# The first five z units, the sums of squares and the norm weights of a hybrid decoder block, arranged anew

## The chip, the core and the metric

The kernel runs on one core of a Trainium2 chip. A core has TensorE (PE, matrix products into PSUM), VectorE (DVE), ScalarE (ACT), GpSimd (POOL) and SyncE (SP, which issues transfers), each with its own queue that it works off in order; they meet at semaphores. Operands lie in SBUF, 128 partitions wide; PSUM has eight banks of 128 x 512 float32. The metric is the time of one execution in microseconds (us); smaller is better.

## The reference

One decoder block on 512 tokens of width 1024, batch 1, depth 1, all float32:

```python
u = rmsnorm(x, norm_mix_g)
proj = u @ w_in     # [q_A k_A v_A z_A a_A b_A | q_B k_B v_B f_B | gate_A gate_B]
# A: causal conv(4) + SiLU on q,k,v; q,k L2-normed; beta = sigmoid(b_A)
#    g = -exp(a_log) * softplus(a_A + dt_bias); gated delta rule in chunks -> o_A
y_A = (rmsnorm(o_A, gdn_norm_g) * silu(z_A)) @ w_proj_gdn
# B: per-head QK RMSNorm, log_f = log_sigmoid(f_B + f_bias),
#    softmax(q k^T / sqrt(d) + c_t - c_s), c = cumsum(log_f), causal -> o_B
y_B = o_B @ w_proj_fox
h = x + (sigmoid(gate_A) * y_A + sigmoid(gate_B) * y_B) @ w_out
out = h + relu(rmsnorm(h, norm_mlp_g) @ w_up)^2 @ w_down
```

The change concerns `u`, the 1024 columns of z_A and the 24 columns of a_A, b_A and f_B ("ab").

## The kernel before, in words

Every float32 product is made of three: a value is split into a high part (rounded to the type that TensorE takes in one pass, a cast on ScalarE) and a low part (what the cast left, a subtraction on VectorE), and high x high, high x low and low x high are added in PSUM. x comes transposed, as eight blocks `xt[k]` of 128 channels x 512 tokens; a "unit" of weights is 128 output columns, 128 x 1024 in SBUF, with its eight contraction steps side by side. `load` (L200) issues a unit's transfer, `prefetch_split` (L243) makes its two parts, `unit` (L260) hands it out and keeps both ahead; raw weights have three buffers, the parts four. Transfers go over SP's queue in the order in which the program reaches them. `dense` (L269) makes 24 products of one unit into one PSUM bank; `mmps` (L92) gives out the three banks of the pool `pmm` in rotation, `atps` (L101) those of the other five.

The mean square of a token is only known when all eight blocks are there. So the first part of the projection is made of x times the norm weights `norm_mix_g`, not of u: the loop at L390 splits each block with the weight as scale (L289, L290), squares it on ScalarE (L395) and adds the squares up on VectorE (L397). L400 to L407 go through the eight blocks once for the ab columns (bank 0) and the first two z units (banks 1 and 2). Then `sumsq` (L348) adds over channels with TensorE ("ss"), `inv_rms` (L354) makes 1/rms: scale and offset on VectorE, a power on GpSimd (L345), and a product that spreads it over the partitions ("rb"), copied to SBUF (L364).

After that `normalise` (L410) multiplies each block by rb on GpSimd (L412), splits the result into `uhi` and `ulo` (again L289 and L290) and stores it; `gates` (L467) makes the decay and beta values out of the ab columns, a long chain of small operations with the products "abt", "cum" and "rowsT". Both are generators that advance one piece at each `tick`. Meanwhile `zgate` (L1072) takes z units 2 to 4, still made of x, multiplies by rb (L1081), applies SiLU and stores. From unit 5 on, u is used: the twelve units of the first four DeltaNet heads (`project`, L593, "w_gdn") follow, then the attention branch, the other heads, the projections and the MLP.

A scheduler of the framework sets the order on each engine from the program's order and its own estimates; where two instructions are marked to keep the program's order, it leaves them so.

Of the kernel before, what the change touches and what calls it, by code (L numbers as in the profile page):

```python
# [30 lines left out]
NZX = 5  # L31
# [12 lines left out]
def hybrid_block(tc, a, out):  # L44
# [81 lines left out]

    def tick():
        for t in list(tasks):
            try:
                next(t)  # L130
            except StopIteration:
                tasks.remove(t)
# [67 lines left out]
    def load(n):  # L200
        nme, i = seq[n]
        if nme in FACTOR:
            w, c, s_ = i
            q, old = FACTOR[nme]
            if old is None:
                if w == "w_st":
                    raw = (swp if nme == "P1" else wraw).tile([P, D], F32, tag="raw", name=nm("sraw"))
                else:
                    raw = fresh[2 if nme == "P2" else s_].tile([P, D], F32, tag="raw", name=nm("draw"))
                nc.sync.dma_start(raw, a[w][c, q, s_])  # L210
# [12 lines left out]
        w = 256 if nme == "w_ab" else D  # L223
        raw = wraw.tile([P, D], F32, tag="raw", name=nm("raw"))
        cuts = [slice(0, 512), slice(512, D)] if 0 < n < 3 else [slice(0, w)]
        for c in cuts:
            nc.sync.dma_start(raw[:, c], a[nme][i][:, c])
        raws[n] = raw, cuts
# [14 lines left out]
    def prefetch_split(n):  # L243
        while len(units) < min(len(seq), n):
            raw, cuts = raws[len(units)]
            hi = whl.tile([P, D], F32R, tag="hi", name=nm("hi"))
            if not units:
                h3 = v3(hi[:, 0:512], KT)
                r3 = v3(raw[:, 0:256], KT)
                act.copy(h3[:, :, 0:32], r3)  # L250
                vec.tensor_tensor(h3[:, :, 32:64], r3, h3[:, :, 0:32].bitcast(F32), op=ALU.subtract)
                units.append((hi, None))
                continue
            lo = whl.tile([P, D], F32R, tag="lo", name=nm("lo"))
            for c in cuts:
                act.copy(hi[:, c], raw[:, c])  # L256
                vec.tensor_tensor(lo[:, c], raw[:, c], hi[:, c].bitcast(F32), op=ALU.subtract)  # L257
            units.append((hi, lo))
# [23 lines left out]
    def split(src, scale=None, dst=None):  # L282

        hi, lo = dst or (page(F32R, "hi")[:, :], page(F32R, "lo")[:, :])
        if scale is None:
            act.copy(hi, src)
            vec.tensor_tensor(lo, src, hi.bitcast(F32), op=ALU.subtract)
        else:
            act.activation(hi, src, AF.Copy, scale=scale)  # L289
            vec.scalar_tensor_tensor(lo, src, scale, hi.bitcast(F32),  # L290
                                     op0=ALU.mult, op1=ALU.subtract)
# [12 lines left out]
    for _ in range(NWARM):  # L304
        mm(pw[:, 0:P], ones, ones, start=True, stop=True)
# [42 lines left out]
    def sumsq(sqs):  # L348
        pss = atps("ss")
        for c in range(NCH):  # L350
            mm(pss[:, c * 64:(c + 1) * 64], sqs[:, cs(c)], ones[:, 0:64], start=True, stop=True)
        return pss

    def inv_rms(pss, rs, rb):  # L354


        for c in range(NCH):
            vec.tensor_scalar(rs[:, c:c + 1], pss[:, c * 64:c * 64 + 1], 1.0 / D, EPS, op0=ALU.mult, op1=ALU.add)
# [3 lines left out]
        for c in range(NCH):  # L362
            mm(prb[:, cs(c)], rs[:, c:c + 1].to_broadcast([P, P]), ident, start=True, stop=True)
# [25 lines left out]
    sqs = page(s="proj")  # L389
    for k in range(KT):  # L390
        xs.append(split(xt[k], mix_g[:, k:k + 1], dst=spots[2 * k:2 * k + 2] if k < 3 else None))
        if k < 2:
            prefetch_split(2 + k)
        sq = page(s="sq") if k else sqs
        act.activation(sq, xt[k], AF.Square)  # L395
        if k:
            vec.tensor_tensor(sqs, sqs, sq, op=ALU.add)  # L397
    first = [unit("w_ab"), unit("w_z"), unit("w_z")]
    fps = [mmps() for _ in first]
    for k in range(KT):  # L400
        w = first[0][0][:, k * 64:(k + 1) * 64]
        mm(fps[0][:64, :], w, xh(k), start=(k == 0), stop=False)
        mm(fps[0][:64, :], w, xl(k), start=False, stop=(k == KT - 1))
        for (hi, lo), o in zip(first[1:], fps[1:]):
            mm(o, hi[:, cs(k)], xh(k), start=(k == 0), stop=False)
            mm(o, hi[:, cs(k)], xl(k), start=False, stop=False)
            mm(o, lo[:, cs(k)], xh(k), start=False, stop=(k == KT - 1))  # L407
    pss = sumsq(sqs)
# [58 lines left out]
    def gates(ps):  # L467
        abT = page(s="abT")
        act.copy(abT[:64, :], ps[:64, :])
# [38 lines left out]
        mm(pc[:, 0:64], upper, gf[:, :, :].rearrange("p a b -> p (a b)"), start=True, stop=True)  # L508
# [558 lines left out]


    gt = start(gates(fps[0]))
    tick()  # L1070
    tick()
    def zgate(h):  # L1072
        if h < 2:
            ps = fps[1 + h]
        elif h < NZX:
            ps = dense("w_z", xh, xl)
        else:
            ps = dense("w_z", uh, ul)
        z = page(s="proj")
        if h < NZX:  # L1080
# [440 lines left out]
```

## Time and profile before

| | us |
|---|---|
| median of 3 runs (lowest to highest) | 979.46 (979.27 to 979.87) |
| the profiled execution | 979.09 |
| its span, first to last instruction | 977.3 |

All rows come from this execution, at a granted TensorE clock of 1.00. In a row of the timeline stand the start, the duration, the engine, the line, the operation with output and input, the shapes, the count, and in brackets the idle time before it and who ended it. "PEld" is TensorE's loading of weights, "SPq" SP's queue. `xs`, `hi` and `lo` hold parts of x or of weights, `ulo` the low part of u, `sq` and the first `proj` squares and their sum.

### The profile page before, as it was taken

Reading aid. Unit: us, or ns where it says so; the run is one execution under the profiler, and the core shown is the slowest. Engines: PE = TensorE matmul, PEld = TensorE weight load, DVE = VectorE, ACT = ScalarE, POOL = GpSimd, SP = SyncE. Lnnn points to the kernel's source line nnn. Section 1 sums busy time; section 2 is a strip of 40 time slices with the busy share of each in tenths; the row PEclk is TensorE's granted clock in tenths of the full one; section 3 lists DMA queues with packets and bytes.
Section 4 is the critical chain, followed back from the end, with each engine's and each line's share of the span. In section 5 each row is a group of like instructions: output and inputs, shape, how many; then the busy total and the mean of one; then the engine's idle time right before and its main releaser. Section 6 shows DMA issues by size and latency. Waiting matters only on the chain.

```text
span 977.3 us, 17204 instructions
## 1 busy us (share of the span) xinstructions
PE 968.0 (99%) x6532; PEld 871.9 (89%) x6532; DVE 709.4 (73%) x1206; ACT 617.8 (63%) x1079; POOL 219.5 (22%) x220
## 2 busy tenths in 40 slices
PE   8999999999999999999999999999999999999998
PEld 6788899998888999999998888889989989988986
DVE  6877777656577799855656534889896697698596
ACT  7778654766764787868567412668755765666761
POOL 1503220202313423521320014412121121121110
PEclk9999999999999999999999999999999999999999
DMA  7646872475675987757888726678698888889883
GB/s 267 210 146 191 236 179 88 130 256 175 156 210 163 194 155 169 174 120 175 252 172 234 258 88 191 113 180 173 184 197 192 194 168 203 184 170 205 187 175 110
DMA packets 97634, 176.50 MB, mean 181 GB/s; under 512 B 8160, under 2 KB 53376, under 8 KB 97552
## 3 DMA queue, kind: packets, MB, share of 16 engines
q1 hardware_dynamic: 83088, 122.92, 40.6%
q0 software_dynamic: 14464, 52.49, 30.8%
q8 instruction: 51, 0.84, 0.4%
q14 instruction: 31, 0.25, 0.1%
HBM read 154.34 MB, written 21.04 MB: 179 GB/s over the span
## 4 chain that ended last, share of the span: by engine, by line
PE 91%; ACT 3%; DVE 2%; issue 2%; DMA 1%; POOL 0%; SPq 0%; ACTq 0%; POOLq 0%; DVEq 0%
PE mlp L1172 36%; PE st L1012 13%; PE mm L279 7%; PE mm L276 7%; PE mm L275 7%; PE fx L965 2%; PE fx L962 2%; PE fx L963 2%; PE fo L945 2%; PE sc L920 2%; PE pT L936 1%; ACT hi L256 1%; PE kq L648 1%; PE kk L640 1%; DMA row<-oad 1%
## 5 line engine op out<-in xcount | busy, mean ns | idle before, releaser
L1403 ACT CAST hi<-draw 128x1024 fp32r<-128x1024 f32 x124 | 130.1, 1050 | 118.4 <-PE mlp L1172 101.5
L1410 DVE TENSOR_TENSOR lo<-draw,hi 128x1024 fp32r<-128x1024 f32 x124 | 151.2, 1221 | 44.9 <-ACT hi L1403 42.1
L256 ACT CAST hi<-raw 128x1024 fp32r<-128x1024 f32 (+1 forms) x62 | 62.7, 1020 | 77.6 <-PE mm L276 48.6
L1172 PE MATMUL mlp<-hi,shi 128*128 128x512 f32 x280 | 109.5, 391 | 0.1
L1172 PE MATMUL mlp<-hi,slo 128*128 128x512 f32 x280 | 109.1, 390 | 0.0
L1172 PE MATMUL mlp<-lo,shi 128*128 128x512 f32 x280 | 109.0, 389 | 0.0
L257 DVE TENSOR_TENSOR lo<-raw,hi 128x1024 fp32r<-128x1024 f32 (+1 forms) x62 | 75.4, 1222 | 28.3 <-ACT hi L256 13.6
L1172 PE MATMUL mlp<-slo,hi 128*128 128x256 f32 x448 | 90.3, 283 | 0.0
L1172 PE MATMUL mlp<-shi,lo 128*128 128x256 f32 x448 | 90.3, 283 | 0.0
L1172 PE MATMUL mlp<-shi,hi 128*128 128x256 f32 x448 | 90.3, 283 | 0.0
L276 PE MATMUL mm<-ulo,hi 128*128 128x512 f32 x216 | 84.9, 394 | 1.2 <-DVE ulo L290 1.2
L275 PE MATMUL mm<-uhi,hi 128*128 128x512 f32 x216 | 85.2, 396 | 0.0
L257 DVE TENSOR_TENSOR lo<-sraw,hi 128x1024 fp32r<-128x1024 f32 x49 | 61.6, 1257 | 23.5 <-ACT hi L256 20.1
L1172 PEld LDWEIGHTS mlp<-shi,hi 128*128 128x128 f32 x448 | 70.6, 192 | 0.9
L256 ACT CAST hi<-sraw 128x1024 fp32r<-128x1024 f32 x49 | 51.3, 1047 | 30.7 <-PE st L1012 14.8
L1172 PEld LDWEIGHTS mlp<-shi,lo 128*128 128x128 f32 x448 | 69.9, 192 | 0.0
L1172 PEld LDWEIGHTS mlp<-slo,hi 128*128 128x128 f32 x448 | 69.8, 192 | 0.0
L1172 PEld LDWEIGHTS mlp<-hi,shi 128*128 128x128 f32 x280 | 52.6, 188 | 11.1 <-issue 0.7
L1172 PEld LDWEIGHTS mlp<-lo,shi 128*128 128x128 f32 x280 | 52.6, 188 | 11.1
L1172 PEld LDWEIGHTS mlp<-hi,slo 128*128 128x128 f32 x280 | 52.6, 188 | 10.3
L600 DVE SCALAR_TENSOR_TENSOR conv<-mm,c_conv,conv 128x511 f32<-128x511 f32 (+2 forms) x72 | 53.5, 744 | 5.6 <-ACT conv L597 4.4
L279 PE MATMUL mm<-uhi,lo 128*128 128x512 f32 x216 | 57.1, 402 | 0.0
(337 smaller groups left out, 2389.7 us busy)
## 6 DMA issues: line engine op xcount, KB each, us to landing
draw<-w_u POOLq DMA_DIRECT2D x32, 512.0 KB, 6.0
draw<-w_d POOLq DMA_DIRECT2D x32, 512.0 KB, 6.0
sraw<-w_st POOLq DMA_DIRECT2D x28, 512.0 KB, 6.0
draw<-w_d SPq DMA_DIRECT2D x26, 512.0 KB, 4.3
raw<-w_gdn SPq DMA_DIRECT2D x24, 512.0 KB, 4.3
draw<-w_u SPq DMA_DIRECT2D x24, 512.0 KB, 4.5
sraw<-w_st SPq DMA_DIRECT2D x21, 512.0 KB, 5.2
hd<-hd SPq DMA_DIRECT2D x34, 256.0 KB, 5.5
```

What stands on the lines that cost most here:

```text
L256: act.copy(hi[:, c], raw[:, c])
L257: vec.tensor_tensor(lo[:, c], raw[:, c], hi[:, c].bitcast(F32), op=ALU.subtract)
L275: mm(o, w, rhi(k), start=(k == 0), stop=False)
L276: mm(o, w, rlo(k), start=False, stop=False)
L279: mm(o, lo[:, k * cols:(k + 1) * cols], rhi(k), start=False, stop=(k == KT - 1))
L600: vec.scalar_tensor_tensor(y[:, s:], ps[:, :T - s], cw[:, i:i + 1], y[:, s:], op0=ALU.mult, op1=ALU.add)
L920: mm(psc[:, :n], qT[:, s], kT[:, :n], start=True, stop=True)
L945: mm(po[:, cs(i)], vt[c], st[i][:, cs(c)], start=(c == 0), stop=(c == i))
L1012: mm(o, u, w, start=first and t == 0 and k == 0 and j == 0 and x is hi, stop=x is lo and k == 3, skip_group_check=True)
L1172: return (lambda *args, **kw: tc.keep_in_program_order(f(*args, **kw))) if self.pinned[0] else f
L1403: pact.copy(hi, raws[m][0])
L1410: pvec.tensor_tensor(lo, raws[m][0], hi[:, :].bitcast(F32), op=ALU.subtract)
```

## The change

- The five z units are made side by side. Their weights come as eight blocks `w_zk[k]` of 128 x 640, one for each contraction step with the five units' columns in it (three units as before come later as whole units). Five banks hold the sums: the three of `pmm` and two others; ab has one more. For each k TensorE makes 15 products for z. Those of ab stand ahead of z for k below 4; the other four pairs, `ss` and `rb` are put between z products at fixed places. All of this, and the products `cum` and `rowsT` of the gates, are marked to keep the program's order.
- Squares: GpSimd makes those of blocks 0 to 2 and adds them up, ScalarE the other five, VectorE adds these and the two sums.
- The gates and `normalise` start inside the z loop (`step`), and all five z evictions (`zgate`, now L1140) come after it.
- The norm weights come as 8 rows of 128 over ScalarE's queue and are transposed by TensorE. Six warming products stand ahead of this and three behind it in the program, in place of ten. Before, they came as columns over GpSimd's queue.
- The low parts of the DeltaNet units 2 to 4 (numbers 11 to 13 in `seq`) are made by GpSimd. The ab weights' cast is VectorE's. Small loads, and those of later weights, stay behind the loads of x. `x_id` and `fqs` are made later in the program, and one operation over four columns takes the place of four in `inv_rms`.

Three places where the order moved; names carry a buffer number.

TensorE around the sums of squares. Before (`mm_273` is ab, `mm_274` and `mm_275` are z 0 and 1, `mm_442` z 2):

```order
L403 MATMUL mm_273<-lo_255,hi_200 64x512
L406 MATMUL mm_274<-lo_255,hi_203 128x512
L407 MATMUL mm_274<-hi_254,lo_204 128x512
L406 MATMUL mm_275<-lo_255,hi_212 128x512
L407 MATMUL mm_275<-hi_254,lo_213 128x512
L351 MATMUL ss_340<-ones,proj_197 128x64 x4
L275 MATMUL mm_442<-xs_195,hi_261 128x512
L276 MATMUL mm_442<-xs_195,hi_261 128x512
```

Now (`ab_262` is ab, `mm_263` to `mm_265` and `fp_266` and `fp_267` are the five z units, here at k = 3):

```order
L377 MATMUL ss_364<-ones,proj_200 128x64 x4
L446 MATMUL mm_265<-hi_228,hi_306 128x512
L447 MATMUL mm_265<-lo_229,hi_306 128x512
L448 MATMUL mm_265<-hi_228,lo_307 128x512
L440 MATMUL ab_262<-hi_233,hi_204 64x512
L441 MATMUL ab_262<-lo_234,hi_204 64x512
L446 MATMUL fp_266<-hi_228,hi_306 128x512
L447 MATMUL fp_266<-lo_229,hi_306 128x512
L448 MATMUL fp_266<-hi_228,lo_307 128x512
L440 MATMUL ab_262<-hi_240,hi_204 64x512
L441 MATMUL ab_262<-lo_241,hi_204 64x512
L388 MATMUL rb_381<-ident,rs 128x128 x4
```

`ss` stood behind all products of eight blocks and now stands inside the fourth; ten products follow before `rb`.

VectorE ahead of the first DeltaNet unit. Before:

```order
L1081 TENSOR_TENSOR proj_373<-mm_274,rb 128x512
L1081 TENSOR_TENSOR proj_402<-mm_275,rb 128x512
L477 TENSOR_TENSOR ab<-abt_377,rs 128x128
L1081 TENSOR_TENSOR proj_493<-mm_442,rb 128x512
L482 TENSOR_TENSOR yy<-ab,c_gdn_dt_bias 128x4x8
L483 TENSOR_TENSOR yy<-ab,c_fox_f_bias 128x4x8
L290 SCALAR_TENSOR_TENSOR ulo_185<-x_120,c_norm_mix_g,uhi_177 128x512
L484 TENSOR_SCALAR yy<-yy 128x4x8
L490 TENSOR_SCALAR beta<-beta 128x32
L487 SCALAR_TENSOR_TENSOR ee<-yy 128x64
```

Now (`lo_508` is the low part of DeltaNet unit 1, `mm_263` the bank of z 0, which is the next one that `mmps` gives to DeltaNet unit 0):

```order
L307 SCALAR_TENSOR_TENSOR ulo_192<-x_127,mix_g,uhi_184 128x512
L272 TENSOR_TENSOR lo_508<-raw_473,hi_507 128x1024
L307 SCALAR_TENSOR_TENSOR ulo_193<-x_128,mix_g,uhi_185 128x512
L307 SCALAR_TENSOR_TENSOR ulo_194<-x_129,mix_g,uhi_186 128x512
L520 TENSOR_TENSOR ab<-abt_484,rs 128x128
L307 SCALAR_TENSOR_TENSOR ulo_195<-x_130,mix_g,uhi_187 128x512
L525 TENSOR_TENSOR yy<-ab,c_gdn_dt_bias 128x4x8
L526 TENSOR_TENSOR yy<-ab,c_fox_f_bias 128x4x8
L533 TENSOR_SCALAR beta<-beta 128x32
L527 TENSOR_SCALAR yy<-yy 128x4x8
L534 RECIPROCAL beta<-beta 128x32
L1140 TENSOR_TENSOR proj_551<-mm_263,rb 128x512
```

The first eviction of a z unit stood ahead of all `ulo`, and now stands behind the last one.

GpSimd, from its constants to the multiplication by rb. Before:

```order
L336 COPY mid<-upper 64x128
L337 TENSOR_SCALAR mid<-upper 64x128
L342 TENSOR_SCALAR fqs<-c_fox_q_norm_g 128x1
L345 TENSOR_TENSOR rs<-rs,expo 128x4
L412 TENSOR_TENSOR x_120<-x_120,rb 128x512
L412 TENSOR_TENSOR x_121<-x_121,rb 128x512
```

Now:

```order
L421 TENSOR_TENSOR proj_201<-x_123 128x512
L421 TENSOR_TENSOR sq_220<-x_124 128x512
L423 TENSOR_TENSOR proj_201<-proj_201,sq_220 128x512
L421 TENSOR_TENSOR sq_225<-x_125 128x512
L423 TENSOR_TENSOR proj_201<-proj_201,sq_225 128x512
L1147 TENSOR_SCALAR fqs<-c_fox_q_norm_g 128x1
L371 TENSOR_TENSOR rs<-rs,expo 128x4
L453 TENSOR_TENSOR x_123<-x_123,rb 128x512
L453 TENSOR_TENSOR x_124<-x_124,rb 128x512
L453 TENSOR_TENSOR x_125<-x_125,rb 128x512
```

Five tensor operations of 128 x 512 have come in ahead of the power; behind the eight multiplications there now also stand three subtractions of 128 x 1024.

The diff, cut to its core:

```diff
-NWARM = 10
+NWARM = 6
 NZ1 = 5
+SQA = 3
+POOL_LO = range(11, 14)
...
-    seq = [("w_ab", 0)] + [("w_z", i) for i in range(NZ1)]
+    seq = [("w_ab", 0)] + [("w_zk", k) for k in range(KT)]
...
             for c in cuts:
-                act.copy(hi[:, c], raw[:, c])
-                vec.tensor_tensor(lo[:, c], raw[:, c], hi[:, c].bitcast(F32), op=ALU.subtract)
+                i = act.copy(hi[:, c], raw[:, c])
+                if len(units) < 3:
+                    pin(i)
+                eng = pool if len(units) in POOL_LO else vec
+                eng.tensor_tensor(lo[:, c], raw[:, c], hi[:, c].bitcast(F32), op=ALU.subtract)
...
+    mix_row = page(s="mixr")[0:KT, 0:P]
+    nc.scalar.dma_start(mix_row, a["norm_mix_g"])
...
+    warm_up(NWARM)
+    pg_ = atps("mixg")
+    nc.tensor.transpose(pg_[:, 0:KT], mix_row, ident[0:KT, 0:KT])
+    mix_g = const([P, KT], "mix_g")
+    act.copy(mix_g, pg_[:, 0:KT])
+    warm_up(3)
...
-    mix_g = small_in("norm_mix_g", [P, KT], nc.gpsimd)
+    AHEAD = {0: 2, 1: 3, 3: 4, 7: 5}
     for k in range(KT):
-        nc.sync.dma_start(xt[k], a["xT"][k])
-        if k < 2:
-            prefetch_raw(2 + k)
-    prefetch_raw(4)
+        last = pin(nc.sync.dma_start(xt[k], a["xT"][k]))
+        if k in AHEAD:
+            prefetch_raw(AHEAD[k])
+    anchor.append(last)
...
+    def square(k):
+        sq = sqp if k == 0 else sqs if k == SQA else page(s="sq")
+        if k >= SQA:
+            pin(act.activation(sq, xt[k], AF.Square))
+        else:
+            pool.tensor_tensor(sq, xt[k], xt[k], op=ALU.mult)
+        if 0 < k < SQA:
+            pool.tensor_tensor(sqp, sqp, sq, op=ALU.add)
+        elif k > SQA:
+            vec.tensor_tensor(sqs, sqs, sq, op=ALU.add)
+        if k == KT - 1:
+            vec.tensor_tensor(sqs, sqs, sqp, op=ALU.add)
...
+    abps = atps("ab")
+    fps = [mmps() if i < NMM else atps("fp") for i in range(NZ1)]
+
+    def ab_products(k):
+        w = w_ab[:, k * 64:(k + 1) * 64]
+        pin(mm(abps[:64, :], w, xh(k), start=(k == 0), stop=False))
+        pin(mm(abps[:64, :], w, xl(k), start=False, stop=(k == KT - 1)))
+
+    def z_products(k):
+        hi, lo = unit("w_zk")
+        for i, o in enumerate(fps):
+            pin(mm(o, hi[:, cs(i)], xh(k), start=(k == 0), stop=False))
+            pin(mm(o, hi[:, cs(i)], xl(k), start=False, stop=False))
+            pin(mm(o, lo[:, cs(i)], xh(k), start=False, stop=(k == KT - 1)))
+            yield
...
-        mm(pc[:, 0:64], upper, gf[:, :, :].rearrange("p a b -> p (a b)"), start=True, stop=True)
+        pin(mm(pc[:, 0:64], upper, gf[:, :, :].rearrange("p a b -> p (a b)"), start=True, stop=True))
...
-    gt = start(gates(fps[0]))
-    tick()
-    tick()
+    for k in range(KT):
+        if k < 4:
+            ab_products(k)
+        for i, _ in enumerate(z_products(k)):
+            u = k * NZ1 + i
+            if u == 16:
+                pss = sumsq(sqs)
+                gt = start(gates())
+                step(gt)
+            if 17 <= u < 21:
+                ab_products(u - 13)
+            if u == 21:
+                act.copy(abT[:64, :], abps[:64, :])
+            if u in (18, 32, 36):
+                step(gt)
+            if u > 18:
+                for t in [t for t in tasks if t is not gt]:
+                    step(t)
...
     def zgate(h):
-        if h < 2:
-            ps = fps[1 + h]
-        elif h < NZX:
-            ps = dense("w_z", xh, xl)
-        else:
-            ps = dense("w_z", uh, ul)
+        ps = fps[h] if h < NZ1 else dense("w_z", uh, ul)
         z = page(s="proj")
-        if h < NZX:
+        if h < NZ1:
             vec.tensor_tensor(z, ps, rb, op=ALU.mult)
             ps = z
         act.activation(z, ps, AF.Silu)
         nc.sync.dma_start(zd[h], z)
-        tick()
+        if h >= NZ1:
+            tick()
```

More of the change, by code (lines that the diff above doesn't have):

```diff
@@ L30 @@
 NMM = 3
-NZX = 5
 DECAY_AT = (9, 1)
@@ L62, in hybrid_block, with behind @@
     pat = psx.enter_context(tc.tile_pool(name="pat", bufs=8 - NMM, space=PSUM))
+    pin = tc.keep_in_program_order
+    anchor = []
+    def behind(d):
+        if anchor:
+            order = mybir.DependencyInfo(mybir.DependencyClass.NoSync, mybir.DependencyReason.DATA)
+            tc.add_manual_dep(d.ins, anchor[0].ins.name, order, reason="behind the first loads")
     n_names = [0]
@@ L125, in hybrid_block, with step @@
     tasks = []
+    def step(t):
+        try:
+            next(t)
+        except StopIteration:
+            tasks.remove(t)
     def tick():
         for t in list(tasks):
[L129 to L132, printed above, removed]
+            step(t)
     def finish(*which):
@@ L303, in hybrid_block, with warm_up, small_in @@
     pw = atps("warm")
-    for _ in range(NWARM):
-        mm(pw[:, 0:P], ones, ones, start=True, stop=True)
-    def small_in(name, shape, eng=None):
+    def warm_up(n):
+        for _ in range(n):
+            mm(pw[:, 0:P], ones, ones, start=True, stop=True)
+    warm_up(NWARM)
[4 more added lines that the diff above has]
+    warm_up(3)
+    def small_in(name, shape):
         t = const(shape, "c_" + name)
-        (eng or nc.sync).dma_start(t, a[name])
+        behind(nc.sync.dma_start(t, a[name]))
         return t
@@ L350, in sumsq @@
         for c in range(NCH):
[L351 removed]
+            pin(mm(pss[:, c * 64:(c + 1) * 64], sqs[:, cs(c)], ones[:, 0:64], start=True, stop=True))
         return pss
     def inv_rms(pss, rs, rb):
[L357 to L358 removed]
+        vec.tensor_scalar(rs, v3(pss[:, 0:NCH * 64], NCH)[:, :, 0], 1.0 / D, EPS, op0=ALU.mult, op1=ALU.add)
         rsq(rs, rs)
@@ L388, in hybrid_block @@
         spots += [t[:, i * T:(i + 1) * T] for i in range(n)]
-    sqs = page(s="proj")
+    sqs, sqp = page(s="proj"), page(s="proj")
+    def square(k):
[10 more added lines that the diff above has]
+            vec.tensor_tensor(sqs, sqs, sqp, op=ALU.add)
     for k in range(KT):
-        xs.append(split(xt[k], mix_g[:, k:k + 1], dst=spots[2 * k:2 * k + 2] if k < 3 else None))
+        xs.append(split(xt[k], mix_g[:, k:k + 1], spots[2 * k:2 * k + 2] if k < 3 else None, None if k else pin))
         if k < 2:
             prefetch_split(2 + k)
[L394 to L408, printed above, removed]
+        square(k)
+    w_ab = unit("w_ab")[0]
+    abps = atps("ab")
[11 more added lines that the diff above has]
+            yield
     def normalise():
@@ L465, in rowc, with gates @@
         return t[:, :].unsqueeze(1).to_broadcast([P, NCH, H])
-    def gates(ps):
-        abT = page(s="abT")
-        act.copy(abT[:64, :], ps[:64, :])
+    X_ID = []
+    abT = page(s="abT")
+    def gates():
         yield from inv_rms(pss, rs, rb)
@@ L539, in gates @@
         yield
+        for _ in range(6):
+            yield
         pt = atps("rowsT")
-        nc.tensor.transpose(pt[:32, 0:P], rows[:, 3, :, :].rearrange("p c h -> p (c h)"), ident)
+        pin(nc.tensor.transpose(pt[:32, 0:P], rows[:, 3, :, :].rearrange("p c h -> p (c h)"), ident))
         rowsF = const([32, P], "rowsF")
```

40 lines of the change are left out of this document (24 added, 16 removed).

## The prediction, made before the changed kernel had run

> **What bounds the kernel now.** First the page's busy times and TensorE's waits (microseconds in total, times, longest).
>
> ```profile
> PE 968.0 (99%) x6532; PEld 871.9 (89%) x6532; DVE 709.4 (73%) x1206; ACT 617.8 (63%) x1079; POOL 219.5 (22%) x220
> ...
> PE mm L276 <- DVE ulo L290: 1.2, 2, 0.7
> PE mm L402 <- ACT xs L289: 1.1, 2, 0.6
> PE mm L405 <- ACT hi L256: 0.8, 2, 0.5
> PE mm L275 <- DVE proj L1081: 0.4, 1, 0.4
> ```
>
> TensorE is the bound nearly everywhere, and its longest waits all lie in the first 50 us, which the change rewrites. Behind them TensorE has next to no slack, so what is won or lost there should stay to the end. Next the timeline: when each product starts, what it took, and what it waited for.
>
> ```profile
> 1.05 4.14 PEld L305 LDWEIGHTS warm<-ones 128*128 128x128 f32 x20 [1.05 <-DVE expo L300]
> 5.18 0.72 ACT L289 ACTIVATE xs<-x,c_norm_mix_g 128x512 fp32r<-128x512 f32 x1 [0.60 <-DMA c_norm_mix_g<-norm_mix_g]
> 5.95 0.45 PE L402 MATMUL mm<-xs,hi 128*64 128x512 f32 x1 [0.57 <-ACT xs L289]
> ...
> 43.17 0.39 PE L275 MATMUL mm<-uhi,hi 128*128 128x512 f32 x1
> ...
> 44.53 0.39 PE L275 MATMUL mm<-uhi,hi 128*128 128x512 f32 x1
> 45.43 0.50 PE L276 MATMUL mm<-ulo,hi 128*128 128x512 f32 x1 [0.52 <-DVE ulo L290]
> 46.25 0.40 PE L276 MATMUL mm<-ulo,hi 128*128 128x512 f32 x1
> 47.33 0.50 PE L276 MATMUL mm<-ulo,hi 128*128 128x512 f32 x1 [0.69 <-DVE ulo L290]
> ...
> 52.23 0.39 PE L275 MATMUL mm<-uhi,hi 128*128 128x512 f32 x1
> 54.05 0.61 PE L279 MATMUL mm<-uhi,lo 128*128 128x512 f32 x2
> ```
>
> Eight 512-wide products start between 52.23 and 54.05, so one costs 0.2275 us; the 0.39 of a row overlaps the next. The first DeltaNet unit starts at 43.17 and loses 0.67 (44.53 to 45.43 less one step) and 0.85 (46.25 to 47.33). It is as if it had started at 44.7 without a stall: the change must beat this 44.7.
>
> The third view is of GpSimd and VectorE together, in two places.
>
> ```profile
> L412 POOL TENSOR_TENSOR x<-x,rb x8: 1276/1301/1744, 31.3 to 40.5; 128x512 f32<-128x512 f32 x8
> ...
> 31.25 10.55 POOL L412 TENSOR_TENSOR x<-x,rb 128x512 f32<-128x512 f32 x8 [4.36 <-ACT rb L364]
> 32.61 0.68 DVE L1081 TENSOR_TENSOR proj<-mm,rb 128x512 f32<-128x512 f32 x1
> 35.01 1.82 DVE L290 SCALAR_TENSOR_TENSOR ulo<-x,c_norm_mix_g,uhi 128x512 fp32r<-128x512 f32 x1
> 36.76 1.28 DVE L484 TENSOR_SCALAR yy<-yy 128x32 f32<-128x32 f32 x1
> 41.76 0.74 DVE L290 SCALAR_TENSOR_TENSOR ulo<-x,c_norm_mix_g,uhi 128x512 fp32r<-128x512 f32 x1
> ...
> 601.60 1.22 DVE L257 TENSOR_TENSOR lo<-draw,hi 128x1024 fp32r<-128x1024 f32 x1
> 601.76 2.79 POOL L1230 TENSOR_TENSOR m<-gate,gate 128x256 f32<-128x256 f32 x2 [3.34 <-DVE gate L1228]
> 602.73 2.37 DVE L1204 TENSOR_TENSOR slo<-m,shi 128x512 fp32r<-128x512 f32 x2
> ```
>
> One `ulo` takes 0.74 us alone and 1.82 while GpSimd multiplies; 32 elements take 1.28. An operation that reads PSUM (L1081, 0.68) is not held up. Around 602 large operations stand on both sides and take strict turns: two subtractions last 2.37. So while GpSimd has a queue of tensor operations, each VectorE operation on SBUF pays one **turn**, 1.82 - 0.74 = 1.08 us. Before, mostly tiny operations paid it.
>
> [...]
>
> **The change, part by part.** *Start.* The norm weights now come as rows over ScalarE's queue and are turned by TensorE, behind nine warming products. Ten took 4.14 from 1.05, so nine end at 4.8; the turn and ScalarE's copy add perhaps 0.5 (an estimate from the small operations around them), and the weights are there at 5.3, not 5.18. The first product starts about 6.1, and the second (pinned) waits for the low part of block 0, to 6.85. Nothing is gained here.
>
> *TensorE to the sums of squares.* From 6.85 the order has 58 products ahead of `ss`: 58 x 0.2275 = 13.2, so `ss` is due at 20.05. The scattered waits of 2.3 us in the list above are gone.
>
> *VectorE to the sums of squares.* Prices, each from one row's start to the next row's:
>
> ```profile
> 2.59 5.24 DMA x<-xT
> ...
> 9.28 0.68 DVE L397 TENSOR_TENSOR proj<-proj,sq 128x512 f32<-128x512 f32 x1
> 9.88 1.29 DVE L257 TENSOR_TENSOR lo<-raw,hi 128x512 fp32r<-128x512 f32 x2
> 11.09 0.75 DVE L290 SCALAR_TENSOR_TENSOR xs<-x,c_norm_mix_g,xs 128x512 fp32r<-128x512 f32 x1
> 11.75 0.69 DVE L397 TENSOR_TENSOR proj<-proj,sq 128x512 f32<-128x512 f32 x1
> ...
> 16.81 1.22 DVE L257 TENSOR_TENSOR lo<-raw,hi 128x1024 fp32r<-128x1024 f32 x1
> 17.95 0.68 DVE L397 TENSOR_TENSOR proj<-proj,sq 128x512 f32<-128x512 f32 x1
> ```
>
> An addition costs 0.60, a low part of x 0.66, a weight block's subtraction 0.60 at 512 and 1.14 at 1024, so 0.73 at 640 by the straight line. In VectorE's order, ahead of the last sum and with it, stand 8 low parts (5.28), five weight blocks (0.76 for the cut one, 4 x 0.73) and 5 additions (3.0): 11.96. From 6.1, with 0.4 for block 1 of x (its load landed at 2.59 + 5.24 = 7.83 before), that ends at 18.5. Now GpSimd squares blocks 1 and 2 and adds them: four tensor operations in this stretch, four turns, 4.3 us. The sums are ready at 22.8 and TensorE waits 2.75. Two of seven additions have left VectorE (1.2 us), and three squares ScalarE; the four turns cost VectorE more than it saved.
>
> *From the sums to the first DeltaNet unit.*
>
> ```profile
> 23.13 0.84 PE ss L351 x8
> ...
> 29.66 0.91 PE rb L363 x8
> 30.59 0.59 ACT rb L364
> ...
> 71.49 1.04 POOL L345 TENSOR_TENSOR ssk<-ssk,expo 128x4 f32<-128x4 f32 x1 [3.04 <-DVE ssk L618]
> ```
>
> `ss` ends at 22.8 + 0.84 = 23.7. The power on GpSimd (1.04) hides behind the ten products (2.28) that now stand between `ss` and `rb`; so does the single operation that replaces four on VectorE. `rb` ends at 26.9 and its copy at 27.5. TensorE has 67 products left (15.2) and the small `abt` (0.3): z is through at 42.4, against 43.17.
>
> VectorE now has, from 27.5: two 640-wide subtractions (1.46), two of 1024 (2.28), eight low parts (5.28) and about 0.9 of small work: 9.9. GpSimd multiplies eight blocks at the same time: eight turns, 8.6. Only then comes the first z eviction (0.68 from row 32.61), at 46.0 to 46.7. The unit cannot start before it, because it takes that bank. TensorE waits 46.7 - 42.4 = 4.3. Behind the waiting product are all of TensorE's later ones. Before, three banks rotated and the evictions came long before; that cover is gone.
>
> *The gates.* The product `cum` is now pinned, 46 products (10.5) into the units: due at 57.2.
>
> ```profile
> 51.45 1.26 DVE L500 SCALAR_TENSOR_TENSOR pp<-pp,ee 128x64 f32<-128x64 f32 x5
> 43.19 0.54 DVE L494 RECIPROCAL zz<-zz 128x64 f32<-128x64 f32 x1
> ```
>
> From 46.7 VectorE has four more evictions (2.4), a reciprocal (0.54), some 0.9 of small work and 12 operations of the series at 0.25 (3.0): 53.5. GpSimd now also subtracts three 1024-wide weight blocks, a size with no row; twice the 1.30 is 2.6 at most, 1.3 at least. If each holds VectorE once for 2.0 to 2.4, the gates end near 59.7 and TensorE waits 2.5. Bounds: 0 if they fall into evictions, 4.5 if the casts come later too. I take 2.5. [...]
>
> *At nothing:* `x_id` and now the ab weights' cast stand at VectorE's start, hidden by the wait for the first block (ScalarE's row at 5.18); without it they would cost about 1 us. The eight weight loads move the bytes of five; each is needed 3.4 us (15 products) after the one before, which hides them, and the case without that cover is the last rival. The later row transposes only delay rows that wait for `cum` anyway; their cost, if any, is in the bounds of the gates.
>
> **Sum.** Start at 46.7 against 44.7, +2.0; gates +2.5: +4.5. The profiled execution took 979.09 us (span 977.3), 0.4 under the median 979.46. Forecast 979.1 + 4.5 = **983.6 us**; its own range, with a turn of 0.95 to 1.30 and the gates at 0 to 4.5, is 981 to 988.
>
> **The rivals.** All depends on the turn t: TensorE's wait at `ss` is 4t - 1.55, at the unit 8t - 4.3, neither below 0; the unit starts at 39.6 plus both.
>
> *Turns hide (faster).* If VectorE would be waiting for ScalarE or a load anyway in most turns, t falls under 0.54: the unit starts at 39.6 to 40.2 and the gates are in time. 39.9 - 44.7 = -4.8, or 974.3. For it: PSUM reads are unhurt, and up to 27.5 VectorE waits for data at times. Against it: rows 35.01 and 602.73. It decides below about t = 0.8; between, at 0.6 to 0.7, 976 to 977.
>
> *A quarter of the turns hides (no change).* At t = 0.8 the waits are 1.65 and 2.1, the unit starts at 43.4, and with 1 to 1.5 at the gates it is as before: 979.3, 977.5 to 981.
>
> *Late weight blocks (slower still).* The fifth block's load stands behind the small loads, and its subtraction ahead of the last sum:
>
> ```profile
> 15.25 0.86 SPq L227 DMA_DIRECT2D raw<-w_z  x2
> ```
>
> The load behind the small ones was issued at 15.25 before. If it takes 5.24 like x's, it lands at 20.5, the sums are not late by it; at 8 us they are, by 2: 986 to 988. That the change doesn't do what it says is excluded by the order.
>
> **Chances.** Forecast 0.55, turns hide 0.27, a quarter hides 0.13, late blocks 0.05. What this kernel's measurement can tell is about 0.2%, 2 us. Slower: 0.55 and 0.05, 0.60; faster 0.28; same 0.12. The range leaves out the lower half of "turns hide" and the far end: 975.5 to 987.5.
>
> **What would show it.** Right: `ss` waiting for `proj` by 2 to 3 us near 20; squares, then multiplies, in step with 1.7 us low parts; the first unit waiting for L1140 near 42 to 47; `cum` waiting for `gf`. Wrong: the first unit before 42, or low parts at 0.75 throughout between 27 and 42.

## The result, and the profile after

| | before | changed |
|---|---|---|
| median, us (lowest to highest) | 979.46 (978.39 to 979.87) | 990.39 (990.02 to 990.76) |
| the profiled execution | 979.09 | 990.56 |
| its span | 977.3 | 988.8 |

The ratio is 1.0113 (95% interval 1.0098 to 1.0127): the changed kernel is slower by 10.9 us, where 4.5 was forecast, and lies above the forecast's range of 981 to 988. The span grew by 11.5.

TensorE's waits in the changed kernel (total, times, longest):

```profile
PE ktm L127 <- ACT conv L648: 5.8, 1, 5.8
PE mm L290 <- DVE proj L1140: 3.4, 1, 3.4
...
PE ab L440 <- ACT xs L304: 1.0, 1, 1.0
PE mm L448 <- DVE lo L272: 0.7, 2, 0.5
PE cum L551 <- DVE gf L548: 0.7, 1, 0.7
...
PE ss L377 <- DVE proj L427: 0.2, 1, 0.2
```

The second row is the wait that the prediction put at 4.3. The first, the longest, it did not have at all. Where in time the loss arises is seen at an instruction that comes once for each head of the first group, the transposition `ktm`. TensorE's timeline before, and after:

```profile
65.92 0.60 PE L119 MATMUL ktm<-ident,conv 128*128 128x128 f32 x4
85.53 0.60 PE L119 MATMUL ktm<-ident,conv 128*128 128x128 f32 x4
105.11 0.60 PE L119 MATMUL ktm<-ident,conv 128*128 128x128 f32 x4
123.96 0.60 PE L119 MATMUL ktm<-ident,conv 128*128 128x128 f32 x4
```

```profile
70.50 0.60 PE L127 MATMUL ktm<-ident,conv 128*128 128x128 f32 x4
89.94 0.60 PE L127 MATMUL ktm<-ident,conv 128*128 128x128 f32 x4
115.81 1.11 PE L127 MATMUL ktm<-ident,conv 128*128 128x128 f32 x4 [5.76 <-ACT conv L648]
136.00 0.60 PE L127 MATMUL ktm<-ident,conv 128*128 128x128 f32 x4
```

The differences are 4.6, 4.4, 10.7 and 12.0. So 4.4 is lost up to the second head, 6.3 at the third, and 1.3 between the third and the fourth; later 0.5 comes back.

*Up to the second head.* The changed kernel's timeline:

```profile
21.76 0.68 DVE L427 TENSOR_TENSOR proj<-proj,proj 128x512 f32<-128x512 f32 x1
22.59 1.08 PE L377 MATMUL ss<-ones,proj 128*128 128x64 f32 x8 [0.18 <-DVE proj L427]
...
33.07 3.49 DVE L307 SCALAR_TENSOR_TENSOR ulo<-x,mix_g,uhi 128x512 fp32r<-128x512 f32 x2
43.01 0.39 PE L448 MATMUL fp<-hi,lo 128*128 128x512 f32 x1
46.11 0.63 DVE L1140 TENSOR_TENSOR proj<-mm,rb 128x512 f32<-128x512 f32 x1
46.80 0.67 PE L290 MATMUL mm<-uhi,hi 128*128 128x512 f32 x1 [3.40 <-DVE proj L1140]
52.32 6.48 DVE L543 SCALAR_TENSOR_TENSOR pp<-pp,ee 128x64 f32<-128x64 f32 x8
52.52 4.90 POOL L272 TENSOR_TENSOR lo<-raw,hi 128x1024 fp32r<-128x1024 f32 x2 [4.03 <-ACT hi L268]
59.78 0.41 PE L551 MATMUL cum<-gf,upper 128*128 128x64 f32 x2 [0.67 <-DVE gf L548]
```

The low parts of u go in turns with GpSimd (3.49 for two), the first eviction comes at 46.11, and the first DeltaNet unit starts at 46.80 instead of an effective 44.7. Then something that no term had. TensorE's granted clock in stretches behind the two long waits (from, to, length, busy, clock, DMA):

```profile
47.00:50.00 3.00, 3.00 (x8) 0.50 0.38 141
50.00:51.00 1.00, 1.00 (x5) 0.81 0.02 8
51.00:52.00 1.00, 1.00 (x6) 1.00 0.00 0
...
115.80:119.00 3.20, 3.19 (x10) 0.55 1.02 324
```

Behind the first of them TensorE works at a clock of 0.50 for about 3.3 us, which loses about 1.6 (eight steps of 0.43 instead of 0.23). The 4.4 are thus 2.1 at the first unit, 1.6 of half clock and 0.7 at `cum`.

*At the third head.* The chain that ends in its transposition, in rows picked from the timelines of VectorE, GpSimd, SyncE's queue and ScalarE, first before the change, then after it:

```profile
68.37 0.34 SPq L544 DMA_DIRECT2D rowd<-rowsF  x1
69.71 2.04 SPq L548 DMA_DIRECT2D row<-rowd  x4
79.60 2.09 SPq L548 DMA_DIRECT2D row<-rowd  x1
83.95 0.41 SPq L548 DMA_DIRECT2D row<-rowd  x1
89.26 1.29 POOL L653 TENSOR_TENSOR conv<-conv,row 128x512 f32<-128x512 f32 x1 [6.56 <-DMA row<-rowd]
92.72 0.67 POOL L583 TENSOR_SCALAR_AFFINE_SELECT em<-row 128x512 f32<-128x512 f32 x1
```

```profile
74.50 0.28 DVE L567 COPY rowsT<-rowsT 96x128 f32<-96x128 f32 x1
75.10 0.77 POOL L568 DMA_DIRECT2D rowd<-rowsT  x1 [17.68 <-DVE rowsT L567]
77.12 2.03 SPq L594 DMA_DIRECT2D row<-rowd  x4
83.64 3.39 SPq L590 DMA_DIRECT2D rowd<-rowsF  x1
89.00 1.75 SPq L594 DMA_DIRECT2D row<-rowd  x1
94.44 1.71 SPq L594 DMA_DIRECT2D row<-rowd  x2
97.73 2.35 POOL L699 TENSOR_TENSOR conv<-conv,row 128x512 f32<-128x512 f32 x1 [7.75 <-DMA row<-rowd]
101.02 1.30 POOL L635 TENSOR_TENSOR eb<-em,row 128x512 f32<-128x512 f32 x1
104.88 0.64 POOL L629 TENSOR_SCALAR_AFFINE_SELECT em<-row 128x512 f32<-128x512 f32 x1 [2.57 <-DMA row<-rowd]
105.55 1.28 ACT L633 ACTIVATE em<-em,ngc 128x128 f32<-128x128 f32 x4 [5.03 <-POOL em L629]
115.12 0.63 ACT L648 ACTIVATE conv<-conv 128x512 f32<-128x512 f32 x1
```

The decays are written to DRAM as rows and read back as pages (`row`). Head 0 needs three: two are among the first four requests, the third is the single `row<-rowd` at 79.60 before and 89.00 after, 9.4 later, while TensorE is only 4.4 to 4.6 later. GpSimd's multiplication by that page waits, and `eb` of the second head and `em` of the third stand behind it in GpSimd's order. But what `em` waits for last is its own page: GpSimd stands idle for 2.57 until a `row<-rowd` lands. That page was asked for at 83.95 before and is the first of the two at 94.44 after, 10.5 later. ScalarE waits 5.03 for that `em`, then works without a pause up to the third head's SiLU (L648), which TensorE waits for.

### The profile page after: what moved, and what is told of

It reads as the page before. It is cut to its first block, busy times and chain, and to the rows that moved or that the text cites. A ratio compares the mean times of both kernels' runs of the same rounds, so it can differ in the third digit from the quotient of the medians.

```text
span 988.8 us, 17207 instructions
## 1 busy us (share of the span) xinstructions
PE 970.8 (98%) x6531; PEld 873.8 (88%) x6531; DVE 716.2 (72%) x1201; ACT 613.8 (62%) x1076; POOL 237.3 (24%) x227
## 4 chain that ended last, share of the span: by engine, by line
PE 85%; DVE 4%; ACT 4%; DMA 3%; issue 3%; POOL 1%; SPq 0%; DVEq 0%; ACTq 0%; POOLq 0%
PE mlp L1233 35%; PE st L1060 13%; PE mm L294 6%; PE mm L291 6%; PE mm L290 6%; DMA row<-rowd 3%; PE fx L1013 2%; PE fx L1011 2%; PE fx L1010 2%; PE fo L993 2%; PE sc L968 2%; PE pT L984 1%; DVE ulo L307 1%; PE v L846 1%; ACT hi L268 1%
## 5 line engine op out<-in xcount | busy, mean ns | idle before, releaser
L268 ACT CAST hi<-raw 128x1024 fp32r<-128x1024 f32 (+2 forms) x64 | 63.0, 992 | 69.7 <-PE mm L291 52.2
L272 DVE TENSOR_TENSOR lo<-raw,hi 128x1024 fp32r<-128x1024 f32 (+3 forms) x61 | 77.2, 1270 | 30.3 <-ACT hi L268 18.9
```

What stands on the lines that cost most here:

```text
L268: i = act.copy(hi[:, c], raw[:, c])
L272: eng.tensor_tensor(lo[:, c], raw[:, c], hi[:, c].bitcast(F32), op=ALU.subtract)
```

## The experiments

Unless it says otherwise, an edit is to the changed kernel. Medians in us, with the ratio to the kernel before on the same chip, whose medians there were 978.27 to 978.77.

| | edit | median | ratio (95%) |
|---|---|---|---|
| e1 | rowsF's write as before | 989.33 | 1.0109 (1.0094 to 1.0124) |
| e2 | e1, rowsT copied by ScalarE | 985.91 | 1.0076 (1.0061 to 1.0091) |
| e3 | a free bank for the first unit | 990.08 | 1.0129 (1.0109 to 1.0149) |
| e4 | no low parts on GpSimd | 983.19 | 1.0049 (1.0034 to 1.0064) |
| e5 | e3 + e4 | 981.26 | 1.0029 (1.0018 to 1.0039) |
| e6 | e4, squares on ScalarE | 983.18 | 1.0052 (1.0035 to 1.0070) |
| e7 | e2 + e3 | 985.01 | 1.0072 (1.0056 to 1.0088) |
| e8 | e5, squares on ScalarE | 981.27 | 1.0034 (1.0022 to 1.0046) |
| e9 | e5, gates issued earlier | 983.01 | 1.0040 (1.0026 to 1.0053) |
| e10 | e9 + e1 | 979.28 | 1.0008 (0.9999 to 1.0017) |
| e11 | kernel before, rows 2 us late | 981.55 | 1.0025 (1.0016 to 1.0035) |
| e12 | kernel before, rows 5.6 us late | 980.54 | 1.0019 (1.0009 to 1.0028) |

### e1 and e2: the rows of the decays

e1 takes out the extra yields, e2 also moves the copy.

```diff
-        for _ in range(6):
-            yield
         pt = atps("rowsT")
```

> The changed kernel without the six extra yields ahead of the second row transposition, so that the write of rowsF stands ahead of the first four row requests on SyncE again, as before the change, and not between kn's and vb's stores behind them. Theory LATE ROWS: the 5.8 us for which TensorE waits at the third head's transposition (L127 on ScalarE's L648) comes from rows that are asked for too late: in the changed kernel the write of rowsF holds SyncE from 83.64 to 87.03, and the request of head 0's third row behind it goes out 9.4 us later than before (89.00 against 79.60) where TensorE itself is only 4.6 later. Without that write in front the request goes out 2 to 3.4 us earlier, the ScalarE wait of 5.0 at em falls to 2 to 3, TensorE's wait to 2.5 to 4, and the time from 990.4 to 987 to 988.5. Rival OWN SHIFT: the wait is the transfers' own time (all of a unit is 4.4 late and the rows' transfers share the engines with the weights), and the place of one 16 KB write changes nothing: 990 to 990.8 with the wait between 5 and 6 us.

```diff
-        vec.tensor_copy(rowsT, pt[:96, 0:P])
+        act.copy(rowsT, pt[:96, 0:P])
```

> As e1, and the copy of the first row transposition (L567) made by ScalarE instead of VectorE, where it stood behind three convolution steps (72.27 to 74.50, 4.3 us after the transposition; before the change 2.2 us after). The rows then go to DRAM at about 72.5 instead of 75.10. Theory LATE ROWS: both delays gone (2.6 here, 2 to 3.4 from e1), so TensorE's wait of 5.8 falls to 0 to 1.5 and with it the half clock behind it (1.3 us): 983.3 to 985.5. Rival OWN SHIFT: 990 to 990.8, the wait stays over 4 us. If e1 moves nothing and this does, the rows' start counts and SyncE's queue does not.

In e1 the third row of head 0 was asked for at 87.36 and the wait at the third head fell from 5.8 to 3.2, as LATE ROWS has it; but half clock followed as before (0.50 from 116 to 118), the execution stood 0.7 later already at `cum`, and the time moved by nothing that the intervals tell apart: 989.33 lies in the range of neither theory. The third head's own page was asked for at 94.90, no earlier than in the changed kernel. In e2 (request at 84.84, rows written at 72.44 instead of 75.10, the third head's own page at 92.69) the wait fell to 2.1 and the time to 985.91, somewhat above what LATE ROWS expected (983.3 to 985.5, with a wait of at most 1.5) and outside OWN SHIFT. Half clock remained:

```profile
112.40:115.30 2.90, 2.90 (x9) 0.50 1.02 297
```

So the rows cost at least about 4 us of the 10.9, and a wait of 2.1 still costs its half clock.

### e3: the wait at the first DeltaNet unit

```diff
-    fps = [mmps() if i < NMM else atps("fp") for i in range(NZ1)]
+    fps = [mmps() if i < 2 else atps("fp") for i in range(NZ1)]
...
+        keep = pin if n_dense[0] == 1 else lambda i: i
...
-            mm(o, w, rhi(k), start=(k == 0), stop=False)
+            keep(mm(o, w, rhi(k), start=(k == 0), stop=False))
...
```

> The changed kernel with z unit 2 accumulated in one of the five other banks instead of the third mm bank, so that the first DeltaNet unit has a free bank and needs no eviction; the products of that unit are kept in program order behind the z products, and TensorE's order is that of the changed kernel. The wait of 3.4 us at L290 for L1140 and the half clock behind it (eight products at 0.43 us, 1.6 us) should go: the first DeltaNet unit starts at 43.3 to 43.6 instead of 46.80. Theory GATES NEXT: cum is pinned 46 products behind, and gf is not ready before 59.6 whatever TensorE does, because VectorE's pp chain takes turns with GpSimd's 128x1024 subtractions until 58.8; cum then waits about 5 us where it waited 0.7, the clock falls there, and of the 5.0 us nothing or up to 1 us is kept: 989.5 to 991. Rival START WAIT: what the start loses is lost for good, and the time falls by 4.5 to 5.5: 985 to 986.

TensorE's timeline and waits of e3:

```profile
42.99 0.39 PE L294 MATMUL mm<-uhi,hi 128*128 128x512 f32 x1
...
59.20 0.69 PE L555 MATMUL cum<-gf,upper 128*128 128x64 f32 x2 [5.62 <-DVE gf L552]
```

The unit starts at 42.99, without a wait or half clock (1.00 for the first 50 us), and everything is given back at `cum`, which waits 5.62 for gates that hardly moved. GATES NEXT holds; START WAIT falls. Until the gates are earlier, the wait at the first unit costs nothing.

### e4: the low parts back to VectorE

```diff
-POOL_LO = range(11, 14)
+POOL_LO = range(0)
```

> The changed kernel with the low parts of weight units 11 to 13 on VectorE again instead of GpSimd (squares and normalising multiplications stay on GpSimd). VectorE does three subtractions of 1.22 more (3.7), but the pp chain of 6.48 for 8 falls to about 1.9 and ee from 1.92 to 0.2 (6.3 less): gf ready about 57. TensorE's order moves with it: cum stands 23 products (5.3 us) further back, and the first row transposition 23 products further back too. Theory LATE ROWS: cum waits for nothing (0.7 gained), but the rows start about 5 us later by the order, of which 2 to 3 come back since their copy no longer stands behind three convolution steps: the third head's wait grows from 5.8 by 1 to 3, and the time becomes 991 to 993.5. Rival TURNS: what the change costs is VectorE's turns with GpSimd, and without them around the gates it is 2 to 5 us faster: 985.5 to 988.5.

Faster than either theory expected. VectorE's series in e4:

```profile
53.01 0.48 DVE L543 SCALAR_TENSOR_TENSOR pp<-pp,ee 128x64 f32<-128x64 f32 x2
...
58.24 0.73 DVE L543 SCALAR_TENSOR_TENSOR pp<-pp,ee 128x64 f32<-128x64 f32 x3
```

An operation of the series takes 0.24. The eight that took 6.48 in the changed kernel were not slow alike:

```profile
L543 DVE SCALAR_TENSOR_TENSOR pp<-pp,ee x8: 225/226/2461, 52.3 to 58.6; 128x64 f32<-128x64 f32 x8
```

The median is 226 ns and the longest took 2461. Two of the eight (2.42 and 2.46 us) were held, each by one of GpSimd's two subtractions. In e4 these turns are gone. But VectorE has the subtractions and a convolution in between instead, and the gates end at 59.8, no earlier than in the changed kernel (59.6). So it is not the turns that were worth 7 us. What went is the wait at the third head (0.6 left): the rows' first request is at 77.65 (77.12 in the changed kernel), but in this order only two stores stand on SyncE between it and the request of head 0's third row, at 84.79 instead of 89.00; the third head's own page is asked for at 89.90 instead of 94.44. LATE ROWS was right about the mechanism and wrong about which request counts. The second to fourth head of e4 stand 4.6 behind the kernel before (90.11, 109.72 and 128.59 against 85.53, 105.11 and 123.96). That is the forecast's 4.5 in size and not in kind: `cum` waits for nothing, the first unit starts at 46.20, 1.5 behind the effective 44.7, and behind its wait come thirteen products at half clock, which lose 2.6:

```profile
46.20:51.90 5.70, 5.70 (x13) 0.50 0.54 175
```

### e5 and e7: the free bank again

e5 makes the edits of e3 and e4, e7 those of e2 and e3.

```diff
+    fps = [mmps() if i < 2 else atps("fp") for i in range(NZ1)]
+POOL_LO = range(0)                                # e5
+        act.copy(rowsT, pt[:96, 0:P])             # e7
```

> e3 and e4 together: a free bank for the first DeltaNet unit, and the low parts of units 11 to 13 on VectorE. TensorE's order is that of e4. In e4 the start still has the wait of 3.4 for the first eviction and thirteen products at 0.427 us instead of 0.2275 behind it (2.6). Theory START PAYS ONCE THE GATES ARE OUT OF THE WAY: both go, cum is reached at about 58.7 instead of 64.67 and gf (59.64 in e4, with convolution steps between that now come earlier) is ready at 57 to 59.5, so cum waits 0 to 1: e4's 983.2 minus 5 to 6, 977 to 979, which is the kernel before. Rival ROWS AGAIN: the row pages do not move with TensorE and the third head's wait (0.6 in e4) grows to 3 or more: 980 to 982. Rival GATES NEXT, as in e3 (cum waits over 4): 982.5 to 983.5.

> e2 and e3 together (rowsF's write ahead of the row requests, rowsT copied by ScalarE, free bank), the low parts of units 11 to 13 still on GpSimd. If the wait at cum is VectorE's turns with GpSimd (GATES NEXT), it stays at 5 to 5.6 us as in e3 with half clock behind it, and only the rows' gain of e2 is kept: 985 to 986.5. If the two gains of e3 and e2 add up (no common limit), 980.5 to 982.

e7: `cum` waits 5.8, the wait at the third head is 0.9, and 985.01 says again that with the gates where they are the bank is worth nothing. e5: the order puts `cum` 23 products later, it waits 0.6, and 1.9 us of the 5 that the start gains are kept. The rest is given back at the second and third head (1.2 and 1.4), where the rows are late again. So 981.26 lies in the range of ROWS AGAIN (980 to 982), which had expected one wait of 3 or more. The wait of 1.4 brought no half clock. e5's windows around it:

```profile
107.00:108.00 1.00, 0.63 (x5) 1.00 0.69 171
108.00:110.00 2.00, 2.00 (x12) 1.00 1.05 332
```

### e6 and e8: the squares

```diff
-SQA = 3
+SQA = 0
...
-        sq = sqp if k == 0 else sqs if k == SQA else page(s="sq")
+        sq = sqs if k == SQA else sqp if k == 0 else page(s="sq")
...
-        if k == KT - 1:
+        if k == KT - 1 and SQA:
```

> e4, and all eight squares on ScalarE with their sums on VectorE, as before the change, so that GpSimd issues no tensor operation before the normalising multiplications. Theory TURNS AT THE START: the three VectorE operations that ran beside GpSimd's squares (2.82 for two, 1.52, 1.92 where 0.7 to 0.9 is usual) lose 3 us, and TensorE's early waits (1.2 at the sums, 0.3 and 0.7 at low parts) go: 981 to 982.5. Rival SCALARE LOADED: three more squares of 0.73 each and two more additions stand ahead of high parts that TensorE waits for, the sums come 1 to 3 us later than in e4, and the time is 984 to 986.

> e5 with the squares of e6: GpSimd then has only the normalising multiplications of what the change gave it. By TURNS AT THE START it is 1 to 2 us faster than e5: 975.5 to 977.5, faster than the kernel before. By SCALARE LOADED it is 1 to 3 us slower than e5: 979 to 981.

983.18 against e4's 983.19, and 981.27 against e5's 981.26: both theories fall. VectorE's sums end at 22.00 in e6 against 21.88 in e4, and at 22.52 in e8 against 22.44 in e5: without the turns VectorE has two more additions and one more weight block ahead of the last sum, and in e6 waits 1.3 for ScalarE. It comes out even; that part of the change does nothing to the time.

### e9 and e10: the gates earlier

```diff
-                act.copy(abT[:64, :], abps[:64, :])
-            if u in (18, 32, 36):
+                pin(act.copy(abT[:64, :], abps[:64, :]))
+            if u in (18, 24, 28):
                 step(gt)
-            if u > 18:
+            if u > 21:
...
-            split(xt[k], mix_g[:, k:k + 1], dst=(uh(k), ul(k)))
+            split(xt[k], mix_g[:, k:k + 1], dst=(uh(k), ul(k)), keep=pin)
```

> e5, and the gates' steps issued earlier among the z products: ab's transposition back (abt) behind product 24 of 40 instead of 32, the rest behind 28 instead of 36; ScalarE copies abT ahead of the high parts of u. cum's place moves 14 products forward among TensorE's. e5 still waits 0.6 at cum, 1.2 and 1.4 at the second and third head, and stands 2.3 us behind the kernel before by the fourth head (126.29 against 123.96). Theory LATE ROWS: with gf and so the rows some 3 us earlier against TensorE, the two waits at the heads shrink to under 0.5 each and cum's goes: 978 to 979.3, no different from the kernel before. Rival VECTORE FULL: the gates' 4 us on VectorE now stand between the last ulo and the first evictions, and TensorE waits 2 us or more at the first or second DeltaNet unit instead: 981 to 983.

> e9 without the six extra yields, so that rowsF's write stands ahead of the first four row requests again and not between the third and the fourth. If the place of that write costs by itself what it did in e1 (2.6 us of wait at the third head), this is 0.3 to 1 us faster than e9; if only the rows' start counts, the two are equal within 0.5. Either way not faster than the kernel before by more than 0.5 us, since before the change TensorE waits for only some 4 us in all: 977.7 to 979.3.

In e9 `cum` came at 56.15 without a wait (59.54 in e5) and TensorE waited at neither of the first units, so VECTORE FULL fails in its mechanism though 983.01 lies in its range; the whole 4.0 is at the third head, with half clock behind it (0.50 from 109 to 111), and LATE ROWS (978 to 979.3) misses too. In e10 rowsF's write stands ahead of the row requests, and the wait is 1.4, without half clock (1.00 from 103 to 108):

```profile
PE ktm L127 <- ACT conv L650: 1.4, 1, 1.4
...
PE ss L381 <- DVE proj L431: 0.4, 1, 0.4
```

That is 979.28, no different from the kernel before by its interval, and 3.7 less than e9, far more than the 0.3 to 1 expected. Head 0's third row was asked for 0.7 earlier (79.34 against 80.01), its multiplication ran 2.1 earlier (88.00 against 90.09) and the third `em` 3.4 earlier (93.62 against 97.06). The last step is again the third head's own page, for which GpSimd waits 2.40 in e9 and not at all in e10. Its request follows that of head 0's third row on SyncE, and between the two stand two weight loads in e9 and one in e10. There are two as well in the changed kernel, e1, e2, e3 and e7, and one in the kernel before and in the other experiments; GpSimd's `em` waits 0.4 us or more for its page in the six with two and at most 0.13 in the rest. So the same edit takes a weight load out from between the requests in e10 and not in e1. That this order alone makes the difference was not tested.

### e11 and e12: late rows alone, in the kernel before

```diff
-        nc.gpsimd.dma_start(rowd[0:3, :, :, :].rearrange("k c h t -> (k c h) t"), rowsT)
+        for _ in range(2):                        # e12: 3
+            nc.gpsimd.dma_start(rowd[0:3, :, :, :].rearrange("k c h t -> (k c h) t"), rowsT)
```

> The kernel before the change, with the first rows written to DRAM twice, one write waiting for the other: the rows are there about 2.5 us later (0.6 of issue and 1.9 to the landing), and TensorE, VectorE, ScalarE and SyncE keep the order of the kernel before to the instruction. Theory LATE ROWS: rows that are late against TensorE cost time by themselves. In e1 the request of head 0's third row was about 2.5 us late against TensorE and the third head waited 3.2; here the same lateness without any other part of the change gives a wait of 1 to 3 at a head, with or without half clock behind it: 979.5 to 982.5. Rival SLACK: before the change the rows have 2 us or more in hand (ScalarE waits there only 0.56 for em), and nothing moves: 978 to 979.

> As e11 with three writes, the rows about 5 us late; on ScalarE and SyncE some instructions are ordered anew around them (one convolution's Silu behind the em exponentials, one weight load ahead of the row requests). Theory LATE ROWS: a wait of 3 to 6 at a head and half clock behind it (1.3), 982.5 to 985.5. Rival SLACK: under 980.

TensorE's waits of e11:

```profile
PE ktm L119 <- ACT conv L603: 1.2, 1, 1.2
...
PE vtm L119 <- ACT conv L603: 0.6, 1, 0.6
```

Rows 2.1 us later (first request 71.78 against 69.71), with every engine's order as before, cost 2.8 us (1.6 to 3.4 by the interval): the kernel before has no slack there, and SLACK falls. e12's rows are 5.6 later and cost no more, 1.8 (0.9 to 2.7): some of VectorE's, ScalarE's and SyncE's work was ordered anew around them, its waits are 1.1 and 0.6, and its time lies between the two expectations. What late rows cost hangs on the order as much as on the lateness. Over all runs (lateness: how much later than before, less how much later the second head is):

| | e4 | e6 | e12 | e10 | e5 | e8 | e7 | e11 | e2 | e3 | e1 | e9 | changed |
|---|---|---|---|---|---|---|---|---|---|---|---|---|---|
| request of head 0's third row, us | 0.6 | 0.2 | 1.5 | 0.4 | 0.6 | 1.1 | -0.3 | 2.0 | 1.1 | 3.2 | 2.7 | 1.8 | 5.0 |
| the third head's `em`, us | 0.8 | 1.2 | 1.4 | 1.6 | 1.8 | 1.9 | 2.5 | 2.7 | 3.7 | 3.9 | 5.5 | 5.7 | 7.7 |
| wait at the third head's `ktm`, us | 0.6 | 1.0 | 0.6 | 1.4 | 1.4 | 1.0 | 0.9 | 1.2 | 2.1 | 2.3 | 3.2 | 4.0 | 5.8 |

The waits follow the request of head 0's third row only loosely, and the third head's `em` closely.

## Why the prediction was half right

The direction was right. The time was not: 990.39 lies above 988, and above the 987.5 given with the chances.

*Right, to a few tenths.* VectorE's sums were forecast for 22.8 and were there at 22.44 (that the four turns cost VectorE more than it saved is not borne out: without the squares on GpSimd the sums come no earlier in e6 and e8); the first eviction for 46.0 to 46.7 (46.11 to 46.74), the first unit for 46.7 (46.80), the gates for 59.7 (59.63). The turn of 1.08 is seen in 3.49 for two `ulo`, 1.01 each over 0.74. The range's turn of 1.30, the whole of a multiplication on GpSimd (1301 ns before), is shown by no `ulo`: the longest in the changed kernel took 1.79, a turn of 1.05. That each subtraction "holds VectorE once for 2.0 to 2.4" is seen in the two held operations of the series. What is lost up to the second head is 4.4 against the forecast sum of 4.5. That e4 took 983.19, close to the forecast 983.6, is luck: its loss has no wait at `cum` and 2.6 of half clock. "Turns hide" and "a quarter hides" fall with the 46.80, "late weight blocks" with the sums at 22.44.

*Right in the sum by two errors that cancel.* "TensorE waits 2.5" at `cum` became 0.7, because TensorE was late itself: half clock behind the 3.4 us cost 1.6. The clock had been read only as 1.00 before, where the longest single wait behind the warm-up was 0.7, and a forecast with a wait of 4.3 in it had to ask for the clock behind it. "TensorE waits 2.75" at `ss` became 0.2, since TensorE came 2.4 later than "due at 20.05": the first products started 0.4 later, some 1.5 went at and behind two waits for low parts of weights (0.7 in the list), and a product took 0.233 here (36 steps between 13.64 and 22.02), not 0.2275. The first DeltaNet unit waits for VectorE, so this changed nothing there. The range's lower end was added up wrongly as well: by the prediction's own formula a turn of 0.95 and gates at 0 give 979.6, not 981; the measured time lies beyond the other end.

*The step that failed:* "The later row transposes only delay rows that wait for `cum` anyway; their cost, if any, is in the bounds of the gates." The bounds of the gates ended at `cum`. Behind it the rows go through a copy, a write, requests in SyncE's order, GpSimd and ScalarE, and come out as 5.8 us of wait and 1.3 of half clock at the third head, 50 us after `cum`, the last place that the prediction looked at. The edit was costed at nothing with a cover (the wait for `cum`) that it had named and not followed: what is queued behind the moved write on SyncE was not asked, and the row of ScalarE's timeline before the change that hints at rows near their limit was not read:

```profile
93.42 0.70 ACT L587 ACTIVATE em<-em,ngc 128x128 f32<-128x128 f32 x2 [0.56 <-POOL em L583]
```

ScalarE waits there for the same mask. That nothing behind `cum` covers late rows is shown by e11: 2.1 us of lateness alone cost 2.8. How the 6.3 divide between the moved write, the copy behind three convolution steps and the order of SyncE's other transfers is not settled: e2 removes the first two and recovers about 4.

*Why no version gained.* In the lists of TensorE's waits, those that the two kernels do not share sum to 3.8 before (1.2, 1.1, 0.8, 0.4, 0.3) and to 2.8 in e10 (1.4 at the third head, 1.0 at the first product, 0.4 at `ss`). So the most favourable version had 1.0 us of waits to gain, and its span, 977.5 against 977.3, does not show even that; where the 1.0 went is not settled.

## What to carry to other kernels

When TensorE is moved by a few microseconds, follow what it feeds as well as what feeds it: a page that comes back through DRAM two heads later has its own queue order, and each engine whose order it passes can add to its lateness (here a request was 9.4 us late where TensorE was 4.4 to 4.6). An edit that is costed at nothing because it "waits for something else anyway" needs the first consumer behind that wait named, with its slack from a row. Half clock followed TensorE waits of 2.1 (e2), 2.3 (e3), 3.2 (e1) and 4.0 (e9) at the third head, and none followed 1.4 (e5, e10): a forecast with such a wait in it needs the clock behind it as a term of its own.

## What the runs showed of the hardware

Half clock after short waits. Waits of 2.1 (e2), 3.4 and 5.8 (changed kernel) were each followed by about 3 us at a granted clock of 0.50 to 0.55, which loses 1.3 to 1.6; after 1.4 (e5, e10) it stayed at 1.00. The price of one and the same wait varies: behind the 3.4 of e4 the clock was 0.50 for 5.7 us, which loses 2.6. The row of e2 has 0.50 from 112.40 to 115.30, so here a gap of 2.1 was enough.

A small transfer held SyncE. Issuing rowsF's 16 KB write took 0.34 us ahead of the row requests and 3.39 behind them (68.37 before, 83.64 after). The stores and requests around it took 1.8 to 2.4 there, which points to the place, behind four row pages and two more transfers, rather than to the write; in e9, behind three of the pages, it took 0.50.

GpSimd's subtraction of 128 x 1024 took 2.37, and two in a row 4.90, inside the prediction's bounds of 1.3 and 2.6. A VectorE operation of 0.23 that met one took 2.42 and 2.46, so it was held for nearly the whole of it.
